# One 512-column product for the values of both residue groups, and the order of the first slots behind it

## The chip, the cores and the metric

The kernel runs on one core of a Trainium2 chip. The metric is device time in microseconds of one execution, the median of several runs; lower is better. The core's engines have these names in the profile: PE is TensorE (with PEld, its weight loads), DVE is VectorE, ACT is ScalarE, POOL is GpSimd, SP is SyncE. Each has its own instruction list and runs it in order; semaphores hold an instruction back until what it needs from another engine or a DMA is there.

## The reference

One layer of a hybrid decoder on x of 512 positions x 1024 channels, in float32. It normalizes x, multiplies it with one wide matrix W_in, and splits the result among three mixers, whose gated outputs are merged; a SwiGLU follows, and a last normalization. The change touches mixer A, dilated window attention of 12 heads in three groups of 4:

```python
A_GROUPS = ((128, 1), (512, 4), (2048, 16))
for g, (window, dilation) in enumerate(A_GROUPS):
    sl = slice(g * A_HEADS_PER_GROUP, (g + 1) * A_HEADS_PER_GROUP)
    o, lse = dilated_window_attention(qa[:, :, sl], ka[:, :, sl], va[:, :, sl],
                                      dilation, window // dilation, rel_bias[:, sl])
    ...
wts = jax.nn.softmax(jnp.stack(lses, axis=0), axis=0)
o_a = jnp.sum(wts[..., None] * jnp.stack(outs, axis=0), axis=0)
```

Group 0 sees the last 128 positions. Groups 1 and 2 gather keys at stride 4 and 16. Head j of each group is combined with head j of the others through the softmax denominators.

## The kernel before

The layer runs as one long list of matmuls, with the transposed activations x (8 tiles of 128 channels x 512 positions) kept in SBUF. Every float32 product is three matmuls in a rounded format: a number is a high part plus a rest, and `mm3` (L195) adds high x high, low x high and high x low. So x stands as xhi and xlo, a weight chunk of 128 x 1024 as whi and wlo. `stage_g` (L164) brings a chunk: SyncE loads wraw, ScalarE casts whi, and GpSimd (for most chunks) or VectorE subtracts wlo. `chunk_plan` (L56) lists the chunks in the order in which the products take them, two ahead of use.

A projection (`project`, L225; `fa`, L663) holds the weights still and lets the 512 positions pass: 8 x 3 matmuls of 512 columns. `fa(half, i, w)` computes queries (w=0) or keys (w=1) of a pair of heads, and `q_tiles` (L470) and `k_tiles` (L492) split them into the tiles qh, ql, qq and kk on ScalarE and VectorE; with `scaled` false they first multiply by the norm (qt, kt: `unscaled`, L462). In `values_g` (L410) it is x that is held still and the 256 columns of a group's value weights that pass: 4 position blocks x 8 x 3 = 96 matmuls of 256 columns. VA[0] takes contiguous positions. VA[1] and VA[2] need the positions by residue class, every fourth one: `by_class` (L406) reads x at stride 4 as weights. `values_out` (L429) splits the values into v tiles.

A slot is one head j of the three groups. `la(j)` gives its steps of logits (`class_logits` L556 for groups 1 and 2, `head_logits` L522 for group 0); `weave` (L200) sets such steps between the matmuls of a product. `wa(d)` (L690) takes the exponentials on ScalarE and sends the statistics through DRAM (exch): ScalarE's queue issues the stores, SyncE's the loads that bring them back transposed. `wa2(d)` (L709) combines them on VectorE (mm, df, wd, ds, rd, ff) and scales P. `ta(d)` gives steps that transpose P (ph, pl and pp tiles), and `xa(d)` multiplies P with the values (L647, L765). `renorm` (L909) scales a second copy of x (xt) and splits it (hi, lo) into XN, the normalized x which later projections take. The order of all of it around the change is written out by hand in the list at L940 to L966; each engine's instruction order follows from a scheduler that works on it.

Of the kernel before, what the change touches and what calls it, by code (L numbers as in the profile page):

```python
# [30 lines left out]
OFF_QA, OFF_KA, OFF_VA = 0, A_W, 2 * A_W  # L31
# [24 lines left out]
def chunk_plan():  # L56

    plan = []

    def a(h, i, w):  # L60
        plan.append(("ma", (OFF_QA, OFF_KA)[w], A_PAIRS[h][i]))

    def v(off, g):
        plan.extend(("v", off + g * 256, kh) for kh in range(2))

    def c(m, w):
        plan.append(("m", "w_in", (OFF_QC, OFF_KC)[w] + m * 128))

    def b(m):
        plan.append(("m", "w_in", OFF_XB + m * 128))  # L70
        plan.append(("m", "w_in", OFF_GB + m * 128))

    gates = [("m", "w_in", OFF_GT + n * D + m * 128) for m in range(8) for n in range(3)]

    def g(place):
        for _ in range(EARLY[place]):
            plan.append(gates.pop(0))

    for n in (0, 1):
        a(0, n, 0)  # L80
        a(0, n, 1)
    v(OFF_VA, 0)
    v(OFF_VA, 1)
    a(0, 2, 0)
    a(0, 2, 1)
    v(OFF_VA, 2)
    for n in range(2):
        a(1, n, 0)
        a(1, n, 1)
    a(1, 2, 0)  # L90
    g("a2")
    a(1, 2, 1)
    g("a3")
    v(OFF_VC, 0)
    g("v0")
    v(OFF_VC, 1)
    c(0, 0)
    g("v1")
    c(0, 1)
    g("c0")  # L100
    c(1, 0)
    c(1, 1)
    g("c1")
    for m in (2, 3):
        c(m, 0)
        g("l1" if m == 2 else "l3")
        c(m, 1)
        g("l2" if m == 2 else "l4")
    b(0)
    g("b0")  # L110
    plan.append(("lru",))
    for m in range(1, 4):
        b(m)
    g("b1")
    np_ = 0
    for m in range(8):
        while gates and 24 - len(gates) < 3 * m + 3 + G_LEAD:
            plan.append(gates.pop(0))
        while np_ * 8 < (m + 1) * 10:
            plan.append(("p", np_))  # L120
            np_ += 1
    for m in range(8):
        plan.append(("m", "w_out", m * 128))
    for m in range(FT):
        plan.append(("m", "w_gu", m * 128))
        plan.append(("m", "w_gu", FFN + m * 128))
    for k in range(FT):
        plan.append(("d", k))
    return plan


def layer_kernel(tc, x0p, xT, wts, tab, oneh, msk, idn, gfin, out):
    nc = tc.nc
    plan = chunk_plan()
    pos = [0]

    with (
# [17 lines left out]
        def bank(s="ps"):  # L155
            return pp.tile([128, 512], F32, name=uid(s), tag="ps")
# [38 lines left out]
        def mm3(o, lh, ll, rh, rl, start, stop):  # L195
            nc.tensor.matmul(o, lh, rh, start=start, stop=False)  # L196
            nc.tensor.matmul(o, lh, rl, start=False, stop=False)  # L197
            nc.tensor.matmul(o, ll, rh, start=False, stop=stop)  # L198

        def weave(gen, n, steps=(), first=0):  # L200

            done = 0
            i = 0
            while True:
                try:
                    next(gen)
                except StopIteration as e:
                    for st in steps[done:]:
                        st()
                    return e.value  # L210
                i += 1
                while done < len(steps) and i - first >= (done + 1) * (n - first) / (len(steps) + 1):
                    steps[done]()
                    done += 1
# [51 lines left out]
        X = []  # L266
        parts = [stage_g(), stage_g()]
        for k in range(KT):
# [8 lines left out]
            g = xp[:, 512 + k : 513 + k]  # L277
            hi = slot(F32R, "xhi")
            nc.scalar.activation(hi, xt, AF.Copy, scale=g)
            lo = slot(F32R, "xlo")  # L280
# [125 lines left out]
        def by_class(ap):  # L406

            return ap.rearrange("p (i c) -> p c i", c=4)

        def values_g(perm=False, act=X):  # L410
            ch = [chunk("v"), chunk("v")]
            pss = []
            for tb in range(4):
                if tb % 2 == 0:
                    pss.append(bank())
                o = pss[-1][:, (tb % 2) * 256 : (tb % 2) * 256 + 256]
                t = slice(tb * 128, (tb + 1) * 128)
                for k in range(8):
                    hi, lo = ch[k // 4]
                    c = slice((k % 4) * 256, (k % 4) * 256 + 256)  # L420
                    xs = [by_class(x)[:, tb, :] if perm else x[:, t] for x in act[k]]
                    mm3(o, xs[0], xs[1], hi[:, c], lo[:, c], k == 0, k == 7)
                    yield
            return pss

        def values_mm(steps=(), first=0, perm=False, act=X):
            return weave(values_g(perm, act), 32, steps, first)

        def values_out(pss, perm=False, scaled=False):  # L429
            res = []  # L430
            for tb in range(4):
                o = pss[tb // 2][:, (tb % 2) * 256 : (tb % 2) * 256 + 256]
                o4 = o.rearrange("p (h e) -> p h e", h=4)
                v = slot(F32R, "v")
                v4 = v.rearrange("p (h two e) -> p h two e", two=2, e=E)
                if scaled:
                    nc.scalar.copy(v4[:, :, 0, :], o4)
                    nc.vector.tensor_sub(v4[:, :, 1, :], o4, f32(v4[:, :, 0, :]))
                    res.append(v)
                    continue  # L440
                rt = r_tok[:, tb + 4 * perm : tb + 4 * perm + 1]
                nc.scalar.activation(v4[:, :, 0, :], o4, AF.Copy, scale=rt)
                nc.vector.scalar_tensor_tensor(
                    v4[:, :, 1, :], in0=o4, scalar=rt, in1=f32(v4[:, :, 0, :]),
                    op0=ALU.mult, op1=ALU.subtract,
                )
                res.append(v)
            return res
# [212 lines left out]
                qk[pair[n] + (w,)] = t[n]  # L661

        def fa(half, i, w, steps=(), first=0):  # L663
            scaled = half == 1
            ea(project(XN if scaled else X, "ma", steps, first), half, i, w, scaled)

        def st_part(st, s, o):
# [241 lines left out]
        def renorm(ks):  # L909
            for k in ks:  # L910
                xt = x_again[k]
                nc.vector.scalar_tensor_tensor(xt, in0=xt, scalar=prm[:, k : k + 1], in1=rb,
                                               op0=ALU.mult, op1=ALU.mult)
                XN.append(split(xt))
# [25 lines left out]
        VA.append(values_out(weave(va0, 32)))  # L940
        reload()
        d0, st = la(0)
        VA.append(values_out(values_mm(st, 0, True), True))
        wa(d0)
        renorm(range(4))
        fa(0, 2, 0)
        renorm(range(4, 8))
        fa(0, 2, 1)
        wa2(d0)
        d1, st = la(1)  # L950
        VA.append(values_out(values_mm(st, 8, True), True))
        st = ta(d0)
        fa(1, 0, 0, st)
        wa(d1)
        fa(1, 0, 1)
        xa(d0)
        fa(1, 1, 0)
        wa2(d1)
        fa(1, 1, 1)
        st = ta(d1)  # L960
# [283 lines left out]
def _pack_weights(inp):  # L1244
    f = np.float32
    w = {n: np.asarray(inp[n])[0] for n in ("w_in", "w_out", "w_gu", "w_down", "p_a", "p_b", "p_c")}
    pk = []
    for m in range(8):
        for n in ("p_a", "p_c", "p_b"):
            a = w[n][:, m * 128 : m * 128 + 128]  # L1250
            pk.extend(a[k * 128 : k * 128 + 128] for k in range(a.shape[0] // 128))
    plan = chunk_plan()
    out = np.zeros((len(plan), 128, 1024), f)
    for i, c in enumerate(plan):
        if c[0] == "v":
            _, off, kh = c
            a = w["w_in"][kh * 512 : kh * 512 + 512, off : off + 256]
            out[i] = a.reshape(4, 128, 256).transpose(1, 0, 2).reshape(128, 1024)
        elif c[0] in ("m", "ma"):
            if c[0] == "m":  # L1260
                a = w[c[1]][:, c[2] : c[2] + 128]
            else:
                a = np.concatenate(
                    [w["w_in"][:, c[1] + (g * 4 + j) * E : c[1] + (g * 4 + j + 1) * E] for g, j in c[2]],
                    axis=1,
                )
            out[i] = a.reshape(8, 128, 128).transpose(1, 0, 2).reshape(128, 1024)
        elif c[0] == "p":
            out[i] = np.concatenate(pk[c[1] * 8 : c[1] * 8 + 8], axis=1)
        elif c[0] == "lru":  # L1270
            for wi, n in enumerate(("lru_wa", "lru_wx")):
                a = np.asarray(inp[n])[0]
                for b in range(8):
                    r, t = (b % 2) * 64, wi * 512 + (b // 2) * 128
                    out[i, r : r + 64, t + r : t + r + 64] = a[b]
        else:
            out[i] = w["w_down"][c[1] * 128 : c[1] * 128 + 128]
    return out
# [41 lines left out]
```

## Time and profile before

| what | value |
|---|---|
| median of 3 runs | 917.45 us (917.18 to 918.51) |
| the profiled execution | 919.07 us |
| its span (first to last instruction) | 917.3 us |
| TensorE busy | 897.8 us, 98% |
| VectorE, ScalarE, GpSimd busy | 473.7, 398.5, 244.4 us |
| HBM | 98 GB/s over the span |

The profiled execution lies 1.6 us above the median, and 1.8 us of its time lie outside its span. Times within the span are counted from its start. Matmuls overlap one another in the records, so the spacing of their starts says what one costs.

### The profile page before, as it was taken

To read this page: it belongs to the slowest core of one execution; us is meant where nothing else is said; L and a number is where in the kernel's file an instruction comes from. 1 tells how busy PE (TensorE), PEld (TensorE's weight loads), DVE (VectorE), ACT (ScalarE), POOL (GpSimd) and SP (SyncE) were. 2 spreads that over 40 slices of the span, in tenths; PEclk is the share of its full clock that TensorE was granted. 3 is DMA by queue.
4 is the path that set the end of the run, shared out by engine and by line. 5 is a ranking of instruction groups with operands and counts; after the bars stand their busy time and mean duration, and the time that the engine had idled before them with its cause. 6 is when DMAs were issued, how large, how long until landed. Compare 5 with 4: busy or idle time off the path is not lost.

```text
span 917.3 us, 11267 instructions
## 1 busy us (share of the span) xinstructions
PE 897.8 (98%) x4262; PEld 760.7 (83%) x4262; DVE 473.7 (52%) x922; ACT 398.5 (43%) x692; POOL 244.4 (27%) x163
## 2 busy tenths in 40 slices
PE   9999699999999999999999999999999999999996
PEld 7899688998888888878888888888888888888885
DVE  7497766634655666745334544544444444422226
ACT  7356457546666567763223433333232223211113
POOL 1124045337443333456112130211111111100004
PEclk9899799999999999999999999999999999999998
DMA  7243132362322231223322332322222232222302
GB/s 277 80 149 90 42 116 71 104 105 102 109 89 91 78 107 50 88 101 107 104 88 106 118 111 71 100 97 96 98 92 93 93 111 95 93 92 97 110 24 92
DMA packets 40278, 90.27 MB, mean 98 GB/s; under 512 B 13988, under 2 KB 15780, under 8 KB 40224
## 3 DMA queue, kind: packets, MB, share of 16 engines
q1 hardware_dynamic: 34048, 88.26, 29.2%
q10 hardware_dynamic: 5824, 0.98, 0.7%
q8 instruction: 33, 0.54, 0.3%
q0 software_dynamic: 352, 0.33, 0.1%
q14 instruction: 21, 0.17, 0.1%
HBM read 87.34 MB, written 2.20 MB: 98 GB/s over the span
## 4 chain that ended last, share of the span: by engine, by line
PE 88%; DVE 6%; ACT 4%; DMA 1%; issue 1%; DVEq 0%
PE ps L197 23%; PE ps L196 23%; PE ps L198 23%; PE ps L1171 11%; PE ps L647 1%; PE ps L596 1%; DVE gb L886 1%; PE ps L542 1%; PE ps L543 1%; DVE a L881 1%; ACT whi L178 1%; DMA stn<-exch 1%; DVE xc L840 0%; DVE y L1216 0%; ACT junk L1202 0%
## 5 line engine op out<-in xcount | busy, mean ns | idle before, releaser
L178 ACT CAST whi<-wraw 128x1024 fp32r<-128x1024 f32 (+1 forms) x149 | 154.6, 1039 | 279.6 <-issue 104.9
L196 PE MATMUL ps<-hi,whi 128*128 128x512 f32 x520 | 205.6, 396 | 1.1 <-ACT hi L248 1.1
L197 PE MATMUL ps<-lo,whi 128*128 128x512 f32 x520 | 202.8, 390 | 0.2 <-DVE lo L249 0.2
L198 PE MATMUL ps<-hi,wlo 128*128 128x512 f32 x520 | 202.8, 390 | 0.0
L179 POOL TENSOR_TENSOR wlo<-wraw,whi 128x1024 fp32r<-128x1024 f32 x55 | 133.9, 2437 | 234.4 <-ACT whi L178 225.8
L179 DVE TENSOR_TENSOR wlo<-wraw,whi 128x1024 fp32r<-128x1024 f32 (+1 forms) x94 | 116.9, 1244 | 123.9 <-ACT whi L178 123.8
L196 PE MATMUL ps<-uhi,whi 128*128 128x512 f32 x352 | 137.9, 392 | 0.0
L198 PE MATMUL ps<-uhi,wlo 128*128 128x512 f32 x352 | 137.1, 389 | 0.0
L197 PE MATMUL ps<-ulo,whi 128*128 128x512 f32 x352 | 136.9, 389 | 0.0
L198 PEld LDWEIGHTS ps<-hi,wlo 128*128 128x128 f32 x520 | 97.6, 188 | 20.8
L196 PEld LDWEIGHTS ps<-hi,whi 128*128 128x128 f32 x520 | 97.7, 188 | 20.1 <-ACT hi L248 1.5
L197 PEld LDWEIGHTS ps<-lo,whi 128*128 128x128 f32 x520 | 97.8, 188 | 19.1 <-DVE lo L249 0.5
L1145 POOL TENSOR_TENSOR av<-sg,uu 128x512 f32<-128x512 f32 x22 | 45.7, 2079 | 198.5 <-DVE sg L1143 198.5
L198 PEld LDWEIGHTS ps<-uhi,wlo 128*128 128x128 f32 x352 | 66.1, 188 | 13.9
L197 PEld LDWEIGHTS ps<-ulo,whi 128*128 128x128 f32 x352 | 66.1, 188 | 13.6
L196 PEld LDWEIGHTS ps<-uhi,whi 128*128 128x128 f32 x352 | 66.1, 188 | 13.3
L1171 PE MATMUL ps<-whi,lo 128*128 128x512 f32 (+1 forms) x180 | 57.7, 384 | 0.0
L1171 PE MATMUL ps<-wlo,hi 128*128 128x512 f32 (+1 forms) x180 | 57.6, 384 | 0.0
L1171 PE MATMUL ps<-whi,hi 128*128 128x512 f32 (+1 forms) x180 | 57.2, 384 | 0.0
L1141 DVE TENSOR_TENSOR uu<-ps,rb 128x512 f32<-128x512 f32 x22 | 15.2, 690 | 64.9 <-PE ps L198 64.9
L1171 PEld LDWEIGHTS ps<-whi,hi 128*128 128x128 f32 x180 | 33.8, 188 | 6.8
L1171 PEld LDWEIGHTS ps<-wlo,hi 128*128 128x128 f32 x180 | 33.8, 188 | 6.7
(240 smaller groups left out, 1292.1 us busy)
## 6 DMA issues: line engine op xcount, KB each, us to landing
wraw<-in_wts SPq DMA_DIRECT2D x145, 512.0 KB, 3.2
xt<-in_xT SPq DMA_DIRECT2D x15, 256.0 KB, 5.6
bias<-relb SPq DMA_DIRECT2D x8, 256.0 KB, 5.1
xr<-in_xT SPq DMA_DIRECT2D x8, 256.0 KB, 2.6
out<-y SPq DMA_DIRECT2D x7, 256.0 KB, 2.1
wraw<-in_wts SPq DMA_DIRECT2D x4, 256.0 KB, 4.9
bias<-relb SPq DMA_DIRECT2D x4, 128.0 KB, 4.1
bias<-relb SPq DMA_DIRECT2D x8, 64.0 KB, 4.8
```

The source lines that it names most:

```text
L178: nc.scalar.copy(hi[:, cc], raw[:, cc])
L179: eng.tensor_sub(lo[:, cc], raw[:, cc], f32(hi[:, cc]))
L196: nc.tensor.matmul(o, lh, rh, start=start, stop=False)
L197: nc.tensor.matmul(o, lh, rl, start=False, stop=False)
L198: nc.tensor.matmul(o, ll, rh, start=False, stop=stop)
L542: nc.tensor.matmul(bk, qh[:, qc], kk[:, k0 : k0 + nn], start=True, stop=False)
L543: nc.tensor.matmul(bk, ql[:, qc], kk[:, k0 : k0 + nn], start=False, stop=True)
L596: nc.tensor.transpose(bt[:, o : o + 128], p, ident)
L647: nc.tensor.matmul(po[:, o0 : o0 + n], vf(kt), p, start=(i == 0), stop=(i == len(mms) - 1))
L1141: nc.vector.tensor_mul(uu, pu, r2)
L1145: nc.gpsimd.tensor_mul(av, sg, uu)
L1171: nc.tensor.matmul((acc[tb][hf] if o is None else o)[:, cc], l[:, t], r[:, hf * 512 + cc.start : hf * 512 + cc.stop], start=((k == 0 or fi ...
```

## The change

The values of groups 1 and 2 become one product, `class_values_g`. Its weights are chunks of a new kind, "vv": 256 input channels x 512 columns (both groups side by side), four chunks of the same size as before; the two chunks that VA[2] took after fa(0,2,1) are taken here. For each tile k of x the four residue classes are held still in turn, and 512 columns pass into four PSUM banks, one per class: 8 x 4 x 3 = 96 matmuls of 512 columns instead of 2 x 96 of 256. The steps of slot 0's logits are woven into it as they were into VA[1].

The order of the first slots changes with it. VA[2] no longer stands behind fa(0,2,1), so the steps of slot 1's logits are woven into fa(1,0,0) (from its fourth matmul group on); fa(1,0,0) and fa(1,0,1) take the unnormalized X, with the two multiplies qt and kt that go with it; all eight tiles of `renorm` follow wa2(d0); and xa(d0) comes after fa(1,1,0).

```diff
     v(OFF_VA, 0)
-    v(OFF_VA, 1)
+    plan.extend(("vv", OFF_VA + 256, kq) for kq in range(4))
     a(0, 2, 0)
     a(0, 2, 1)
-    v(OFF_VA, 2)
...
+        def class_values_g():
+
+            pss = [bank() for _ in range(4)]
+            for kq in range(4):
+                hi, lo = chunk("vv")
+                for k in (2 * kq, 2 * kq + 1):
+                    c = slice((k % 2) * 512, (k % 2) * 512 + 512)
+                    for tb in range(4):
+                        xs = [by_class(x)[:, tb, :] for x in X[k]]
+                        mm3(pss[tb], xs[0], xs[1], hi[:, c], lo[:, c], k == 0, k == 7)
+                        yield
+            return [[ps[:, g * 256 : g * 256 + 256] for ps in pss] for g in range(2)]
...
         def fa(half, i, w, steps=(), first=0):
-            scaled = half == 1
+            scaled = (half, i) > (1, 0)
...
         d0, st = la(0)
-        VA.append(values_out(values_mm(st, 0, True), True))
+        for outs in weave(class_values_g(), 32, st):
+            VA.append(values_out(outs, True))
         wa(d0)
-        renorm(range(4))
         fa(0, 2, 0)
-        renorm(range(4, 8))
         fa(0, 2, 1)
         wa2(d0)
+        renorm(range(8))
         d1, st = la(1)
-        VA.append(values_out(values_mm(st, 8, True), True))
+        fa(1, 0, 0, st, 3)
+        wa(d1)
         st = ta(d0)
-        fa(1, 0, 0, st)
-        wa(d1)
-        fa(1, 0, 1)
+        fa(1, 0, 1, st)
+        fa(1, 1, 0)
         xa(d0)
-        fa(1, 1, 0)
         wa2(d1)
         fa(1, 1, 1)
```

Three places show what this does to the engines' lists. The first is TensorE's list at the start of the product; before, it held one PSUM tile for one residue class and went through x (tiles xhi_104, xhi_110 and so on):

```order
L196 MATMUL ps_598<-whi_319,xhi_104 128x256
L197 MATMUL ps_598<-wlo_320,xhi_104 128x256
L198 MATMUL ps_598<-whi_319,xlo_106 128x256
L196 MATMUL ps_598<-whi_319,xhi_110 128x256
L197 MATMUL ps_598<-wlo_320,xhi_110 128x256
L198 MATMUL ps_598<-whi_319,xlo_112 128x256
```

Now the same place holds (ps_586 to ps_589 are the four banks of the four classes):

```order
L195 MATMUL ps_586<-whi_319,xhi_104 128x512
L196 MATMUL ps_586<-wlo_320,xhi_104 128x512
L197 MATMUL ps_586<-whi_319,xlo_106 128x512
L195 MATMUL ps_586<-whi_319,xhi_110 128x512
L196 MATMUL ps_586<-wlo_320,xhi_110 128x512
L195 MATMUL ps_587<-whi_319,xhi_104 128x512
L196 MATMUL ps_587<-wlo_320,xhi_104 128x512
L197 MATMUL ps_587<-whi_319,xlo_106 128x512
```

Each matmul passes twice the columns, and the banks are filled in turn, so that all four end at the product's end. The second place is TensorE's list where slot 1's logits begin (kk_889 before, kk_875 now). Before, half of VA[2] still follows them:

```order
L198 MATMUL ps_959<-whi_857,xlo_154 128x256
L542 MATMUL ps_1006<-kk_889,qh_827 128x256
L543 MATMUL ps_1006<-kk_889,ql_828 128x256
...
L543 MATMUL ps_1007<-kk_889,ql_828 128x256
L196 MATMUL ps_1026<-whi_795,xhi_104 128x256
```

Now fa(1,0,0) (ps_979) has ended ahead of them, and all logits of the slot follow, then fa(1,0,1) (ps_1087):

```order
L197 MATMUL ps_979<-xhi_152,wlo_802 128x512
L554 MATMUL ps_999<-kk_875,qh_833 128x256
L555 MATMUL ps_999<-kk_875,ql_834 128x256
...
L555 MATMUL ps_1000<-kk_875,ql_834 128x256
L576 MATMUL ps_1019<-kk_878,qq_839 128x256 x2
L576 MATMUL ps_1025<-kk_883,qq_839 128x256 x2
L576 MATMUL ps_1037<-kk_457,qq_442 128x256 x2
L576 MATMUL ps_1043<-kk_462,qq_442 128x256 x2
L195 MATMUL ps_1087<-xhi_104,whi_843 128x512
```

No product is left to fill in between the steps of the logits. The third place is VectorE's list at slot 1's exchange, where mm is the first step that needs it and the pp tiles are transposed P of slot 0, which TensorE takes in xa(d0):

```order
L612 TENSOR_TENSOR pl_1114<-ps_1109,ph_1113 128x384
L629 TENSOR_TENSOR pp_1127<-ps_1122,pp_1127 128x2x128
L725 TENSOR_TENSOR mm_1238<-stn_970 128x4
L725 TENSOR_TENSOR mm_1257<-stp_971 128x4
L727 TENSOR_TENSOR df_1240<-mm_1238,stn_970 128x4
L728 TENSOR_TENSOR df_1240<-mm_1238,stn_970 128x4
L727 TENSOR_TENSOR df_1259<-mm_1257,stp_971 128x4
L629 TENSOR_TENSOR pp_1130<-ps_1122,pp_1130 128x2x128
L728 TENSOR_TENSOR df_1259<-mm_1257,stp_971 128x4
L629 TENSOR_TENSOR pp_1144<-ps_1139,pp_1144 128x2x128
```

One pp tile is ahead of mm and the others behind it, as before; now the matmuls that take them stand on TensorE behind fa(1,1,0) and in front of nearly all of fa(1,1,1).

## Rows read from the trace of the kernel before

**Rows 1.** The page's first part: busy us (share of span) and instructions of each engine:

```profile
PE 897.8 (98%) x4262; PEld 760.7 (83%) x4262; DVE 473.7 (52%) x922; ACT 398.5 (43%) x692; POOL 244.4 (27%) x163
```

**Rows 2.** The waits of TensorE: us in total, times, longest us:

```profile
PE ps L542 <- DVE kk L512: 8.0, 1, 8.0
```

**Rows 3.** Stretches: us, busy us (x instructions) by engine, granted clock, DMA share, GB/s:

```profile
84.80:104.10 19.30, 11.25 (x50) 11.08 (x49) 14.54 (x41) 11.37 (x24) 2.38 (x1) 0.81 0.20 55
104.10:107.40 3.30, 3.30 (x15) 3.30 (x16) 3.21 (x9) 0.88 (x4) 0.00 (x0) 0.54 0.00 0
107.40:163.60 56.20, 56.20 (x282) 48.94 (x282) 34.49 (x114) 32.70 (x82) 22.78 (x16) 1.00 0.30 89
```

**Rows 4.** The chain that ended last, 86 to 105: start us, us, what:

```profile
86.66 2.54 DMA exch<-stp
...
89.21 4.65 DMA stn<-exch
...
104.09 0.55 PE ps L542
```

**Rows 5.** The timelines of VectorE and ScalarE's queue, 109 to 130: start us, us, what [idle before]:

```profile
109.35 0.89 DVE L567 TENSOR_TENSOR P<-ps,bias 128x256 f32<-128x256 f32 x2 [1.50 <-PE ps L564]
...
113.79 0.75 DVE L567 TENSOR_TENSOR P<-ps,bias 128x256 f32<-128x256 f32 x2 [2.71 <-PE ps L564]
...
120.58 0.37 ACTq L705 DMA_DIRECT2D exch<-stp  x1
...
127.72 1.05 DVE L713 TENSOR_TENSOR mm<-stn 128x4 f32<-128x4 f32 x1 [3.99 <-DMA stn<-exch]
...
129.11 0.75 DVE L617 TENSOR_TENSOR pp<-ps,pp 128x256 fp32r<-128x256 f32 x2
```

**Rows 6.** TensorE's timeline, 49 to 56:

```profile
49.43 0.28 PE L198 MATMUL ps<-whi,xlo 128*128 128x256 f32 x1
49.55 0.39 PE L196 MATMUL ps<-whi,xhi 128*128 128x256 f32 x1
49.78 0.40 PE L197 MATMUL ps<-wlo,xhi 128*128 128x256 f32 x1
...
55.15 0.28 PE L542 MATMUL ps<-kk,qh 128*128 128x256 f32 x1
```

**Rows 7.** Groups of weight loads, 28 to 123: count | busy us, mean ns:

```profile
L198 PEld LDWEIGHTS ps<-whi,xlo 128*128 128x128 f32 x96 | 28.6, 298 | 0.0
...
L197 PEld LDWEIGHTS ps<-xlo,whi 128*128 128x128 f32 x17 | 3.2, 188 | 0.6
```

**Rows 8.** VectorE's timeline, 62 to 100:

```profile
62.15 0.48 DVE L443 SCALAR_TENSOR_TENSOR v<-ps,mixr,v 128x256 fp32r<-128x256 f32 x1
...
64.99 2.06 DVE L912 SCALAR_TENSOR_TENSOR xt<-xt,prm,rb 128x512 f32<-128x512 f32 x3
...
72.20 0.42 DVE L567 TENSOR_TENSOR P<-ps,bias 128x256 f32<-128x256 f32 x1 [2.62 <-PE ps L564]
72.54 2.59 DVE L912 SCALAR_TENSOR_TENSOR xt<-xt,prm,rb 128x512 f32<-128x512 f32 x1
...
90.89 0.68 DVE L467 TENSOR_TENSOR qt<-ps,rq 128x512 f32<-128x512 f32 x1
...
98.79 0.68 DVE L246 TENSOR_TENSOR lo<-xt,hi 128x512 fp32r<-128x512 f32 x1
```

**Rows 9.** GpSimd's timeline, 72 to 117:

```profile
72.19 2.40 POOL L179 TENSOR_TENSOR wlo<-wraw,whi 128x1024 fp32r<-128x1024 f32 x1 [11.73 <-ACT whi L178]
...
116.61 2.39 POOL L179 TENSOR_TENSOR wlo<-wraw,whi 128x1024 fp32r<-128x1024 f32 x1 [26.79 <-ACT whi L178]
```

**Rows 10.** TensorE's timeline, 132 to 164:

```profile
132.58 0.40 PE L196 MATMUL ps<-hi,whi 128*128 128x512 f32 x1
...
138.05 0.39 PE L196 MATMUL ps<-hi,whi 128*128 128x512 f32 x1
...
163.57 0.28 PE L647 MATMUL ps<-ph,v 128*128 128x256 f32 x1
```

More of the change, by code (lines that the diff above doesn't have):

```diff
@@ L408, in by_class, with values_g @@
             return ap.rearrange("p (i c) -> p c i", c=4)
-        def values_g(perm=False, act=X):
+        def class_values_g():
[9 more added lines that the diff above has]
+            return [[ps[:, g * 256 : g * 256 + 256] for ps in pss] for g in range(2)]
+        def values_g(act=X):
             ch = [chunk("v"), chunk("v")]
-            pss = []
+            outs = []
             for tb in range(4):
                 if tb % 2 == 0:
-                    pss.append(bank())
-                o = pss[-1][:, (tb % 2) * 256 : (tb % 2) * 256 + 256]
+                    ps = bank()
+                o = ps[:, (tb % 2) * 256 : (tb % 2) * 256 + 256]
+                outs.append(o)
                 t = slice(tb * 128, (tb + 1) * 128)
@@ L420, in values_g, with values_mm, values_out @@
                     c = slice((k % 4) * 256, (k % 4) * 256 + 256)
-                    xs = [by_class(x)[:, tb, :] if perm else x[:, t] for x in act[k]]
-                    mm3(o, xs[0], xs[1], hi[:, c], lo[:, c], k == 0, k == 7)
+                    xh, xl = act[k]
+                    mm3(o, xh[:, t], xl[:, t], hi[:, c], lo[:, c], k == 0, k == 7)
                     yield
[L424 to L429, printed above, removed]
+            return outs
+        def values_mm(steps=(), first=0, act=X):
+            return weave(values_g(act), 32, steps, first)
+        def values_out(outs, perm=False, scaled=False):
             res = []
-            for tb in range(4):
-                o = pss[tb // 2][:, (tb % 2) * 256 : (tb % 2) * 256 + 256]
+            for tb, o in enumerate(outs):
                 o4 = o.rearrange("p (h e) -> p h e", h=4)
@@ L1258, in _pack_weights @@
             out[i] = a.reshape(4, 128, 256).transpose(1, 0, 2).reshape(128, 1024)
+        elif c[0] == "vv":
+            _, off, kq = c
+            a = w["w_in"][kq * 256 : kq * 256 + 256, off : off + 512]
+            out[i] = a.reshape(2, 128, 512).transpose(1, 0, 2).reshape(128, 1024)
         elif c[0] in ("m", "ma"):
```

## The prediction

> **What bounds the kernel now.** I read the page's first part, the list of what TensorE waited for, the stretches with their granted clock, the chain of waits and the timelines of each engine, in that order. TensorE is busy for 98% of the span [rows 1], and in the list of its waits only one is long, 8.0 us in one piece for a kk tile of VectorE [rows 2]. Everything else is TensorE running its list, so a change can win in two ways: shorten that list, or shorten the wait. The stretches show where both lie: in 84.80 to 104.10 TensorE is busy for 11.25 of 19.30 us, at a granted clock of 0.81; the next 3.30 us run at 0.54, close to the lower of the two levels (1.2 GHz); then 1.00 (2.4 GHz) without a wait up to 163.60 [rows 3]. The first 49.55 us of TensorE's list and all of it from xa(d1) on (163.57 us) are the same in both kernels, so the sum is made between these points.
>
> The wait belongs to a chain of small steps off TensorE. Slot 0's exponentials end, ScalarE issues exch<-stp at 86.66, SyncE reads it back at 89.21, it lands 4.65 later, at 93.86, VectorE starts mm, and its list from there ends in the kk tile that TensorE takes at 104.09 [rows 4]. A second round follows: exch<-stp at 120.58, mm at 127.72, the first pp tile behind it at 129.11 [rows 5]. TensorE had other work then and did not wait.
>
> **Part 1, the product.** Before, groups 1 and 2 take 2 x 96 matmuls of 256 columns with x taken at stride 4 as weights; 24 of them stand between 49.55 and 55.15, 0.233 us each, where 256 columns on contiguous weights need 0.12 (49.43 to 49.55) [rows 6] and 512 columns 0.228 (24 between 132.58 and 138.05) [rows 10]. The reason stands in the weight loads: 298 ns where x is taken by class, 188 where it is contiguous [rows 7]. So the stride, not the columns, paces them, and 512 columns can pass in the time in which 256 do. Now 96 matmuls of 512 columns do both groups. Lower bound of their spacing 0.233 us (the load stays the pace); upper bound 0.341, if the 0.108 us that 256 more columns take (0.228 less 0.12) came on top. I take the lower: on contiguous weights the load hides wholly. TensorE's list then shortens by 96 x 0.233 = **22.4 us** (12.0 at the upper bound).
>
> TensorE: Matmul & The Clock Gate in the Trainium skill (Part 3, The mechanism) speaks against that: weight loads overlap running matmuls only where their row groups differ. By that rule the product would cost the upper bound, 32.7 us and not 22.4. The contiguous rows, 188 ns of load at a spacing of 0.12, do not agree; the case has its chance among the rivals.
>
> **Part 2, the chain to the wait.** The two exchanges stay, in the same order behind each other, so the saving counts only as far as they move. Slot 0's logits are still woven into the product. Before, VectorE got the last of them after 2.62 us of waiting, at 72.20, and its next xt took 2.59 us where a free one takes 0.69 (2.06 for three), for GpSimd's wlo ran from 72.19 for 2.40 [rows 8, 9]: a VectorE step on two SBUF tensors stands still beside one, at a price of up to 1.9 us. After, the last logits come about as early, one more wlo falls beside the xt steps (+1.9), and three v steps of 0.48 and two lo steps leave the stretch (-2.8). I take the issue of exch<-stp as 0.9 us earlier, 85.8, between 84.7 and 86.7; mm 7.2 later [rows 4], **93.0**.
>
> From mm to TensorE it took 10.2 us. Out of it go four lo steps of 0.68 [rows 8] (-2.7; the change puts all eight behind the kk tiles); in come three v's of 0.48 (+1.4) and qt, 0.68 (+0.7). That is 9.6. But two wlo now fall in it, whose casts stand between ScalarE's steps there; before, GpSimd was idle for 26.79 us up to 116.61 [rows 9]. They cost 0 to 3.8; I take 2.4, a little over one. TensorE restarts at **105.0** (102.3 to 107.3), against 104.09. It has then done the whole product, fa(0,2,0), fa(0,2,1) and fa(1,0,0), and has stood for some 12 us (done at 49.55 + 22.4 + 1.9 of slot 0's logits + 3 of waits inside + 3 x 5.47 = 93.3). Before, half of the product for group 2 and fa(1,0,0) still lay ahead.
>
> **Part 3, slot 1's exchange.** From TensorE's restart to the issue of exch<-stp it took 16.5 us [rows 4, 5]. In come the eight lo steps ahead of the logits (+5.4) and qt (+0.7); out goes VectorE's wait for logits woven into the product, 1.50 and 2.71 (-4.2) [rows 5]. That is 18.4, plus one wlo beside the lo steps, 0 to 1.9, of which I take 0.6: 19.0. Issue at **124.0** (120.7 to 127.6), mm 7.1 later at 131.1 and the second pp tile 1.8 behind mm, at **132.9**. Here lies the new wait: xa(d0) needs that tile, which VectorE's list now puts behind mm, and fa(1,1,1) stands behind it on TensorE. fa(1,0,1) ends near 114; fa(1,1,0) can start when slot 1's logits are reduced, 12.9 behind the restart, and TensorE reaches xa(d0) at about 124.4: a wait of 8.5.
>
> **Part 4, on to xa(d1).** fa(1,1,1) began at 138.05 and xa(d1) at 163.57, 25.5 us of work without a wait [rows 10]; six matmuls of xa(d0) come on top (+0.7). After its new wait TensorE runs some 3.3 us at the lower level, as behind the wait of now [rows 3], which loses half of that, 1.6. So 132.9 + 25.5 + 0.7 + 1.6 = 160.7, against 163.57: **-2.9 us**. VectorE's own list keeps up: behind mm it has ql and qq fewer than now, which are done by then, and kt more. The two extra multiplies (2 x 0.68) are the qt above and a kt behind mm, beside TensorE's wait. Weight chunks keep their number and bytes and come two ahead of use, so I cost them at nothing; a late one would hold TensorE within the product, and the wait at 105 would swallow that. Slot 0's later logits take PSUM banks that v steps and earlier logits must free: about 3 us of waits within the product, swallowed in the same way.
>
> **Sum.** -22.4 for the product; +3.0 of waits inside it; +3.8 for the longer wait at 105 (11.8 for 8.0); +2.3 ahead of fa(1,1,0); +8.5 ahead of fa(1,1,1) and +1.6 for the slow start behind it: -3.2, and with the steps rounded above -2.9. The profiled execution took 919.07 us (span 917.3), which gives 916.2; it is 1.6 above the median of the runs, 917.45, so the median becomes **914.5**.
>
> **The rivals.**
> - *GpSimd's wlo miss VectorE.* All of them at nothing and an early issue: restart 102.3, second pp 129.6, xa(d1) at 157.4, 6.2 us gained: 911.3; and 906 if the eight lo steps (5.4) too fall beside other waits. For it: the xt row shows the stall where a step reads two SBUF tensors, and half of VectorE's steps there read PSUM. Against: the casts stand just where they collide.
> - *The whole saving arrives*, 895. That needs slot 0's exchange some 20 us earlier, and from its issue to mm alone go 7. Hardly.
> - *Everything is given back.* All wlo collide: restart 107.3, second pp 136.5, xa(d1) at 164.3, 0.7 later: 918.2, no change that can be told.
> - *Slower: strided weights don't hide behind 512 columns.* The last logits of slot 0 stand behind 72 class matmuls; at 0.341 they come 72 x 0.108 = 7.8 us later, of which the bank waits ahead of them swallow 2. Everything from exch<-stp on is 5.8 later: -2.9 becomes +2.9, 920.3. The gain is gone from a spacing of 0.30 us on, where 72 x 0.067 is 4.9. For it: no row shows a strided load under 512 columns, and its 298 ns are longer than the 228 that they take. Against: contiguous loads of 188 hide under 120.
> - *The change does not do what it says*: the order of instructions shows 96 matmuls fewer, so no.
>
> **How the numbers follow.** A run tells 0.2% from no change, 1.8 us. Forecast (gain of 1.8 to 6) 0.39, wlo missing (6 to 13) 0.18, whole saving 0.04: faster 0.61. Given back, within 1.8: 0.21. Slower 0.18. The range leaves out the whole saving and what lies beyond the ends worked out: 906 (wlo missing, lo steps covered) to 920.5 (strided loads at the upper bound).
>
> **What would show it.** Spacing in the product: 0.23 (right) or towards 0.34. TensorE's waits: one of about 12 us for kk, to near 105, and a second of 5 to 9 ahead of fa(1,1,1), for a pp tile, near 133; the wait for slot 0's v's in the product under 3. exch<-stp near 86 and 124. TensorE busy about 22 us less at a span only 3 shorter. The forecast is wrong if the second wait is missing, if exch<-stp of slot 0 moves by over 3 us, or if a wait after xa(d1) takes the gain.

## The result, and the profile after

| what | before | after |
|---|---|---|
| median | 917.45 us (917.18 to 918.51) | 924.43 us (923.98 to 924.81) |
| ratio to before, 95% interval | | 1.0074 [1.0056, 1.0091] |
| the profiled execution, its span | 919.07, 917.3 us | 924.81, 923.0 us |

The kernel became slower by 0.74%, 7.0 us. Forecast were 914.5 and a range that ended at 920.5. The page's first part after the change, to be held against [rows 1]:

```profile
PE 886.4 (96%) x4166; PEld 744.6 (81%) x4166; DVE 480.8 (52%) x924; ACT 400.6 (43%) x692; POOL 245.9 (27%) x163
```

TensorE has 96 matmuls fewer and is busy 11.4 us less, in a span that is 5.7 us longer. Its timeline in the product (start us, us, what):

```profile
53.14 0.40 PE L197 MATMUL ps<-whi,xlo 128*128 128x512 f32 x1
53.38 0.39 PE L196 MATMUL ps<-wlo,xhi 128*128 128x512 f32 x1
...
77.86 0.39 PE L197 MATMUL ps<-whi,xlo 128*128 128x512 f32 x1
78.09 0.39 PE L195 MATMUL ps<-xhi,whi 128*128 128x512 f32 x1
```

The starts are 0.235 us apart, against 0.233 for 256 columns [rows 6]: the product itself costs half of what it did, and it ends at 78.09. The loads of its strided weights, 49 to 78 (count | busy us, mean ns), are no faster than before (298, [rows 7]) and hide behind the 512 columns:

```profile
L196 PEld LDWEIGHTS ps<-wlo,xhi 128*128 128x128 f32 x31 | 9.7, 313 | 0.2
```

Where the gain went stands in the list of TensorE's waits (total us, times, longest us), to be held against the single 8.0 of [rows 2]:

```profile
PE ps L554 <- DVE kk L524: 12.1, 1, 12.1
PE ps L777 <- DVE df L728: 5.0, 1, 5.0
PE ps L576 <- DVE v L455: 3.1, 1, 3.1
PE ps L576 <- ACT z L907: 2.6, 1, 2.6
...
PE ps L576 <- DVE half L770: 1.0, 1, 1.0
```

The stretches after (us, busy us of each engine, granted clock, DMA share, GB/s) answer to [rows 3]:

```profile
64.14:67.60 3.46, 3.46 (x10) 2.74 (x9) 2.73 (x3) 2.92 (x4) 3.06 (x2) 0.51 1.05 400
...
94.60:106.71 12.11, 0.00 (x0) 0.03 (x1) 11.19 (x22) 5.09 (x8) 5.34 (x2) 0.66 0.25 87
106.71:115.20 8.49, 7.93 (x25) 6.67 (x26) 7.86 (x10) 6.99 (x12) 2.82 (x1) 0.50 0.00 0
...
129.60:134.55 4.95, 0.00 (x0) 0.03 (x1) 0.98 (x8) 0.48 (x3) 1.26 (x1) 0.79 0.69 207
134.55:139.20 4.65, 4.65 (x12) 3.68 (x13) 4.57 (x20) 4.05 (x8) 0.00 (x0) 0.50 0.02 7
139.20:163.21 24.01, 24.01 (x124) 20.32 (x123) 15.80 (x41) 13.92 (x31) 10.65 (x9) 1.00 0.18 67
163.21:182.00 18.79, 17.64 (x124) 16.26 (x122) 7.50 (x32) 9.56 (x30) 4.80 (x2) 1.00 0.45 99
182.00:190.00 8.00, 5.41 (x31) 5.17 (x32) 8.00 (x35) 2.86 (x9) 3.17 (x4) 0.82 0.00 0
```

Two things are to be seen. Up to xa(d1) the gain is spent: waits of 21.8 us for 8.0, and three starts at the lower level (1.2 GHz, 0.50 to 0.51 in the rows: 3.5, 8.5 and 4.65 us, about half of which is lost) for one of 3.3. That is 13.8 and some 6.5 against the product's 22; xa(d1) begins at 163.21, 0.36 earlier than before [rows 10]. And behind xa(d1), where the kernel before has no wait, TensorE stands for 3.7 us, and its clock sinks to 0.82 for 8. The timeline of VectorE there, before and after:

```profile
171.55 0.68 DVE L758 TENSOR_TENSOR half<-ps,half 64x512 f32<-64x512 f32 x1
172.16 1.27 DVE L769 TENSOR_TENSOR hp<-ps,hp 64x512 f32<-64x512 f32 x2
177.10 0.53 DVE L713 TENSOR_TENSOR mm<-stn 128x4 f32<-128x4 f32 x1 [3.67 <-DMA stn<-exch]
```

```profile
180.32 0.16 DVE L725 TENSOR_TENSOR mm<-stn 128x4 f32<-128x4 f32 x1 [7.10 <-DMA stn<-exch]
180.40 0.16 DVE L725 TENSOR_TENSOR mm<-stp 128x4 f32<-128x4 f32 x1
180.59 0.68 DVE L770 TENSOR_TENSOR half<-ps,half 64x512 f32<-64x512 f32 x1
181.27 0.68 DVE L781 TENSOR_TENSOR hp<-ps,hp 64x512 f32<-64x512 f32 x1
```

Before, half and hp of xa(d1) run when TensorE has their products, and mm of slot 2 waits for its exchange behind them. After, mm stands ahead of them, and they wait 9 us for an exchange that they don't need. They free PSUM banks that TensorE takes at 181.33, and GpSimd's and ScalarE's steps behind them (oa, hi, z) hold it once more at 186.75. No line of the diff touches slot 2: the scheduler that turns the program into instruction lists put mm there. In the profiles the stretch from xa(d1) to xa(d2) takes 56.33 us for 50.31; from xa(d2) to the end they agree, 703.49 for 703.42.

### The profile page after: what moved, and what is told of

Its sections match the earlier page's. It is cut to its first block, busy times and chain, and to the rows that moved or that the text cites. A ratio compares the mean times of both kernels' runs of the same rounds, so it can differ in the third digit from the quotient of the medians.

```text
span 923.0 us, 11073 instructions
## 1 busy us (share of the span) xinstructions
PE 886.4 (96%) x4166; PEld 744.6 (81%) x4166; DVE 480.8 (52%) x924; ACT 400.6 (43%) x692; POOL 245.9 (27%) x163
## 4 chain that ended last, share of the span: by engine, by line
PE 76%; DVE 9%; ACT 5%; DMA 5%; issue 4%; POOL 0%; DVEq 0%; ACTq 0%; POOLq 0%; SPq 0%
PE ps L196 20%; PE ps L195 20%; PE ps L197 20%; PE ps L1182 11%; DMA exch<-stp 2%; ACT P L594 1%; PE ps L608 1%; PE ps L659 1%; DMA stn<-exch 1%; DVE xt L924 1%; DVE gb L898 1%; DVE lo L245 1%; PE ps L555 1%; DMA xt<-in_xT 1%; PE ps L554 1%
## 5 line engine op out<-in xcount | busy, mean ns | idle before, releaser
L195 PE MATMUL ps<-hi,whi 128*128 128x512 f32 x504 | 200.2, 398 | 1.1 <-ACT hi L247 1.1
L196 PE MATMUL ps<-lo,whi 128*128 128x512 f32 x504 | 197.6, 392 | 0.2 <-DVE lo L248 0.2
L197 PE MATMUL ps<-hi,wlo 128*128 128x512 f32 x504 | 197.3, 391 | 0.0
L195 PEld LDWEIGHTS ps<-hi,whi 128*128 128x128 f32 x504 | 95.4, 189 | 20.0 <-ACT hi L247 1.6
L197 PEld LDWEIGHTS ps<-hi,wlo 128*128 128x128 f32 x504 | 95.3, 189 | 20.2
L196 PEld LDWEIGHTS ps<-lo,whi 128*128 128x128 f32 x504 | 95.5, 189 | 18.9 <-DVE lo L248 0.5
L1182 PEld LDWEIGHTS ps<-whi,lo 128*128 128x128 f32 x180 | 33.8, 188 | 6.8
```

The lines of the kernel that those rows point to most:

```text
L1182: nc.tensor.matmul((acc[tb][hf] if o is None else o)[:, cc], l[:, t], r[:, hf * 512 + cc.start : hf * 512 + cc.stop], start=((k == 0 or fi ...
```

## The experiments

Every ratio is to the kernel before, measured beside it on the same chip; edits that build on one another were in part measured on different chips. One profile of an execution is less certain than a ratio: the same lists of TensorE and VectorE up to xa(d1) reached it at 159.8 us on one chip and at 164.3 on another (both_first, slot2_load_both).

**Theory A:** the change moves the bound of the first slots from TensorE to VectorE and the two exchanges, and the order that came with it costs more behind xa(d1). **Rivals:** the product itself is at fault, or what is lost behind xa(d1) would be lost in any order.

### VectorE's order at slot 2

`half_first`: wa2(d2) of the changed kernel behind the last hp of xa(d1) in VectorE's list; TensorE's list is left alone.

```diff
+                tail[0] = nc.vector.tensor_add(hp, pc[0:64, :], hp)
...
-        wa2(d2)
+        with tc.issue_after(tail[0].ins):
+            wa2(d2)
```

> The changed kernel with one edge more: VectorE may issue the mm of slot 2's exchange only behind the half and hp steps of xa(d1). TensorE's list is the same. Theory A (the 6 us behind xa(d1) come from VectorE's order: half and hp stand behind an mm that waits for the exchange until 180.3): half runs near 173, TensorE's waits for half (1.0) and hp (0.2) are gone, that for z shrinks from 2.6 to under 1.5, and the time falls by 5 to 7 us, to 917.5 to 919.5. Theory B (the exchange itself, 11.1 us from issue to mm where it was 8.8 before, is what costs, through the P steps and z behind mm): the time falls by 2 us at most, 922 to 925.

Ratio 1.0019 [1.0009, 1.0029]: 0.55% or 5.0 us of the 0.74% are gone. VectorE:

```profile
172.20 0.68 DVE L771 TENSOR_TENSOR half<-ps,half 64x512 f32<-64x512 f32 x1
172.81 1.27 DVE L782 TENSOR_TENSOR hp<-ps,hp 64x512 f32<-64x512 f32 x2
179.85 0.16 DVE L725 TENSOR_TENSOR mm<-stn 128x4 f32<-128x4 f32 x1 [5.78 <-DMA stn<-exch]
```

`before_mm_first` is the mirror: in the kernel before, wa2(d2) is written ahead of xa(d1), and an order-only dependency puts half and hp behind mm of slot 2. Up to xa(d1), VectorE's order stays as it was.

> The mirror of half_first: the kernel before, with slot 2's mm of VectorE put ahead of half and hp of xa(d1), the order that the change had brought with it; TensorE's list is left alone. Theory A (the order at slot 2 costs by itself): half waits for mm, some 177.1 us instead of 171.6, TensorE stalls behind it by 1 to 3.5 us in the stretch 175 to 190, and the time is 1 to 4 us over the kernel before. Rival (the order is harmless where TensorE has the product's 22 us still in it): no difference, within 0.5 us.

Ratio 1.0050 [1.0035, 1.0065]: 4.6 us slower, a little more than expected, without a trace of the change's product. VectorE and then the stretch 182 to 190 look as in the changed kernel:

```profile
179.18 0.16 DVE L713 TENSOR_TENSOR mm<-stn 128x4 f32<-128x4 f32 x1 [6.45 <-DMA stn<-exch]
...
179.45 0.68 DVE L758 TENSOR_TENSOR half<-ps,half 64x512 f32<-64x512 f32 x1
```

```profile
182.00:190.00 8.00, 5.92 (x35) 5.43 (x34) 8.00 (x37) 3.23 (x11) 2.39 (x3) 0.80 0.00 1
```

That is some two thirds of the loss by the ratios: taking the order away gives 5.0 us back, bringing it in alone costs 4.6. In the profiles, 3.6 and 3.9 of it lie between xa(d1) and xa(d2) (56.33 to 52.75, and 50.31 to 54.23), where the order differs; some 1 us lies ahead of xa(d1), where it doesn't. So the order's own price is 3.6 to 5 us.

### The second wait, at slot 1

`pp_first` puts wa2(d1) behind the last pp tile in the same way; `both_first` has both edits.

> The changed kernel with another edge: VectorE may issue the mm of slot 1's exchange only behind the four pp steps of slot 0. The order at slot 2 stays that of the changed kernel. Theory A: TensorE's wait of 5.0 at 134.55 goes, fa(1,1,1) starts near 130.5 and not at 134.6; but slot 1's mm does not come sooner, so VectorE's list behind it stays where it is, TensorE waits later by most of what it won, xa(d1) comes 0.5 to 2 us sooner, and the loss at slot 2 stays: 922 to 924.5. Rival (the 5.0 us are what the change lost): 918.5 to 920.5.

> Both edges together. Theory A: 916 to 919, the gain of half_first and up to 2 us of pp_first. Rival (each wait only hands its time to the next one): not below 921.

1.0065 [1.0046, 1.0085] and 1.0002 [0.9992, 1.0012]. The 5.0 us wait is gone in both, but 0.8 us of time (against the changed kernel, which the intervals don't tell from nothing) and 1.6 (both_first against half_first) are all that comes of it. In pp_first, where slot 2's order is still the new one, TensorE waits 2.4 us for slot 1's P (from 141 us on) and 0.8 for pp tiles instead, and half of xa(d1) runs at 180.04, as late as without the edit.

### The product alone, and the sequence alone

`two_passes`: the changed kernel, but 256 columns at a time, weights passing twice.

```diff
+                        for g in range(2):
+                            c = slice((k % 2) * 512 + g * 256, (k % 2) * 512 + g * 256 + 256)
+                            mm3(pss[tb][:, g * 256 : g * 256 + 256], xs[0], xs[1], hi[:, c], lo[:, c],
+                                k == 0 and g == 0, k == 7 and g == 1)
```

> The changed kernel with the class values' product cut back into two passes of 256 columns, weights passing twice, all else (staging, banks, the sequence of the first slots) as changed; to be held against the changed kernel (924.4 us where the kernel before has 917.5). Theory A (the product's 22 us do pay within the changed sequence, and the new sequence loses more than that): the product ends some 20 us later (96 to 101 instead of 78.1), the logits of slot 1 start 8 to 15 us later than 106.7, and the time is 8 to 18 us over the changed kernel. Rival (the 22 us are hidden in any order): within 3 us of the changed kernel.

Ratio 1.0142 [1.0127, 1.0158]: 0.68% or 6.2 us above the changed kernel, between the two expectations. The product's last matmul begins at 96.08, 18.2 us later, slot 1's logits at 114.78, 8.1 later. The other 10 us stand in the wait at kk, which is 2.0 us where the changed kernel has 12.1; the second wait stays:

```profile
PE ps L779 <- DVE df L730: 5.4, 1, 5.4
...
PE ps L556 <- DVE kk L526: 2.0, 1, 2.0
```

So the change is the sum of two parts: a sequence that costs 1.42% (13 us, the order at slot 2 among them), and a product that gives 0.68% of it back. The product is not at fault.

`xn_renorm_split` keeps the product and puts back two more pieces of the old sequence: `renorm` in halves ahead of fa(0,2,0) and fa(0,2,1), and fa(1,0,·) on the normalized x. Slot 2's order on VectorE comes out as before with it.

```diff
-            scaled = (half, i) > (1, 0)
+            scaled = half == 1
...
+        renorm(range(4))
         fa(0, 2, 0)
+        renorm(range(4, 8))
         fa(0, 2, 1)
         wa2(d0)
-        renorm(range(8))
```

> The changed kernel with a part of the new sequence undone: the eight xt and lo steps again in two halves around fa(0,2,0), and fa(1,0,0) and fa(1,0,1) on the normalized XN, so without the two extra multiplies; the product of 512 columns stays. VectorE's order at slot 2 comes out as half, hp, mm here. Theory A: the eight lo steps (7.1 us between 109.8 and 116.9) leave the chain from TensorE's restart to slot 1's exchange and go into waits before it, slot 1's exchange is issued 3 to 7 us sooner, and with the order at slot 2 right the time is 912 to 917. Rival (the lo steps only move ahead and delay the kk tile by as much): 917 to 920.

Ratio 0.9993 [0.9983, 1.0004]. TensorE now waits 10.5 us for lo tiles, in three pieces, and 2.9 for a hi, where it waited for kk. With the order mended in this way too, a product that is 22 us shorter is worth under 2 us.

### What holds the first slots

`kk_first`: on half_first, VectorE's work that waits for slot 0's exchange stands behind the kk tiles of fa(0,2,1). `before_kk_first`: the same edit in the kernel before.

```diff
-        wa2(d0)
+        with tc.issue_after(last_kk[0].ins):
+            wa2(d0)
```

> On top of half_first: wa2(d0), VectorE's work that waits for slot 0's exchange, stands behind the last kk of fa(0,2,1) in VectorE's list, not ahead of it; TensorE's list is left alone. Theory A (what bounds the stretch is the exchange of slot 0 through VectorE's queue, and the product's saving was turned into the 12.1 us wait at kk): that wait falls to under 2 us, the logits of slot 1 start at 94.6 to 97 instead of 106.2, the store of slot 1's exchange is issued 6 to 10 us earlier (117 to 121), and the time falls by 5 to 11 us against half_first, below the kernel before. Rival (the wait is only handed on, to the eight lo that fa(1,1,0) needs or to slot 1's own exchange): one of those waits grows to 8 us or more and the time moves by less than 2 us.

> The same edge in the kernel before: wa2(d0) behind the last kk of fa(0,2,1). There TensorE waits 8.0 us at kk. Theory A (both kernels are held by slot 0's exchange through kk, the change more so): the wait goes and the time falls by 3 to 8 us against the kernel before, and kk_first ends 3 to 10 us below this kernel, because only then the product's shorter TensorE work counts. Rival (the product's saving is worth nothing in any order): kk_first and this kernel end within 2 us of each other, or kk_first above.

0.9982 [0.9971, 0.9993] and 0.9953 [0.9939, 0.9966], on the same chip. TensorE's longest waits in kk_first:

```profile
PE ps L611 <- issue: 7.0, 1, 7.0
PE ps L781 <- DVE pp L632: 2.4, 2, 1.7
PE ps L625 <- DVE P L602: 2.2, 2, 1.9
```

and in before_kk_first:

```profile
PE ps L545 <- DVE kk L515: 3.7, 1, 3.7
PE ps L196 <- DVE stn L553: 1.5, 1, 1.5
```

The wait at kk falls from 11.7 to 0.9, as theory A had it, and the time by 3.4 us, less than it had. The rest is handed on to the transposes of slot 0's P (L611). The profile names no releaser for that wait; TensorE ends it at 111.56, just behind VectorE's first steps on slot 1's logits (111.04 to 111.46), which stand behind its scaling of slot 0's P (104.98 to 109.70) and two lo steps. So VectorE's list holds TensorE there too; which tile of it isn't shown. The kernel before gains more by the same edit, 4.3 us, and ends 2.7 us *below* kk_first: the second rival of that pair. With slot 0's exchange out of the way on both sides, the change still loses. From slot 0's store to slot 1's it takes 33.9 us in the kernel before (86.66 to 120.58, [rows 4, 5]), 43.4 after the change (83.24 to 126.59), 37.3 in kk_first and 29.6 in before_kk_first. The 9.4 us that the change adds are 1.9 from the store to mm, 4.2 from mm to TensorE's restart and 3.4 from there to slot 1's store. The reading that fits, argued from the lists and not tried by itself: before, two of renorm's eight lo and half of the v tiles ran ahead of slot 0's store and the other six lo ahead of kk, while now all of them lie between the two stores, the lo behind kk; and TensorE has no product left to fill in there.

`renorm_early`, `renorm_early_kk`: on half_first and on kk_first, `renorm` in halves ahead of fa(0,2,0) and fa(0,2,1). `lo_pool_kk`: kk_first with the eight lo of `renorm` on GpSimd.

> On top of half_first: the renormalised x is split in two halves ahead of fa(0,2,0) and fa(0,2,1), where the kernel before has it, not behind wa2(d0). Theory A (the eight lo in 109.8 to 116.9, between TensorE's restart and slot 1's softmax, are what makes slot 1's exchange late): they run ahead of kk, slot 1's store is issued 3 to 7 us earlier than in half_first (119 to 123 instead of 126.1), the wait at L777's line falls to under 2 us, and the time falls by 2 to 5 us. Rival (VectorE's work is only shifted to ahead of kk): the wait at kk grows from 11.7 to 15 us or more and the time moves by less than 1.5 us.

> renorm_early and kk_first together: VectorE has v, lo and kk ahead of the work that waits for slot 0's exchange. Theory A (the stretch is bound by VectorE's list, and the best order fills its idle 86 to 92 us): kk ends by 100, slot 1's store is issued at 114 to 118, and the time is 2 to 6 us below kk_first. Rival (the list is full in any order): store at 119 or later and time within 1.5 us of kk_first.

> kk_first with the eight lo of the renormalised x computed by GpSimd instead of VectorE (0.65 us each on VectorE). Theory A (VectorE's list bounds the stretch 83 to 117 us): some 5 us leave it, slot 1's store is issued 3 to 5 us earlier than 120.6, and the time falls by 1 to 4 us against kk_first. Rival (GpSimd's lo come later than fa(1,1,0) needs them, or slow VectorE beside them): TensorE waits 3 us or more for lo, and the time is that of kk_first or above.

1.0016 [1.0003, 1.0029], 0.9999 [0.9989, 1.0009] and 0.9989 [0.998, 0.9999]: none faster than its base, as the rivals had it; renorm_early_kk ends 1.6 us above kk_first, and in lo_pool_kk the 3 us wait for lo, which the rival named too, is missing. In renorm_early the wait at kk grows to 19.3 us, for the lo steps now stand ahead of it. In lo_pool_kk the lo steps leave VectorE, but its scaling of P takes 4.2 us longer, most of what they took (timelines of VectorE in kk_first, then in lo_pool_kk with its GpSimd):

```profile
104.98 4.72 DVE L602 TENSOR_SCALAR P<-P,ff 128x128 f32<-128x128 f32 x12
```

```profile
102.31 8.89 DVE L602 TENSOR_SCALAR P<-P,ff 128x128 f32<-128x128 f32 x12
```

```profile
102.32 2.41 POOL L178 TENSOR_TENSOR wlo<-wraw,whi 128x1024 fp32r<-128x1024 f32 x1
104.69 5.06 POOL L245 TENSOR_TENSOR lo<-xt,hi 128x512 fp32r<-128x512 f32 x4
```

Slot 1's store goes out at 120.89, no earlier than kk_first's 120.59. None of the three shortened the stretch between the two stores further than kk_first had.

### Bulk loads beside the exchanges

`hold_load`: on half_first, the 512 KB weight load that SyncE issued between slot 0's two exchange loads goes behind both (an order-only dependency on its own queue).

> On top of half_first: the 512 KB weight load that SyncE issued between slot 0's two exchange loads (83.1 us) is issued behind both. Theory A (the weight load beside it lengthens the exchange store from 2.5 to 6.4 us): the store lands within 2.5 to 4.0 us, mm of slot 0 runs at 89 to 90.5 instead of 91.8, TensorE restarts at 103 to 105 instead of 106.2, and the time falls by 1 to 3 us against half_first. Rival (the flight is the store's own, or set by other loads): the store still takes over 5.5 us, restart and time as in half_first within 0.7 us.

Ratio 1.0014 [1.0002, 1.0026], no difference to half_first. The chain of waits in half_first, then in hold_load:

```profile
83.19 6.19 DMA exch<-stp
89.44 2.36 DMA stn<-exch
```

```profile
81.83 4.43 DMA exch<-stp
86.28 2.41 DMA stn<-exch
```

The store lands 1.8 us faster, not as fast as the 2.54 of [rows 4]; mm comes 3.1 us earlier, 1.4 of it because the store was issued earlier, and the wait ahead of fa(1,1,1) grows from 4.9 to 5.9. So, as far as one profile shows it, the load was some of the store's delay, and the chain passes little of it on.

From xa(d1) to xa(d2) TensorE took 50.3 us in the profile of before (163.57 to 213.87) and 52 to 56 in all others, before_kk_first too (52.8). `slot2_load`, `slot2_load_both`, `slot2_load_before_kk` and `slot2_load_kk` hold the load beside slot 2's exchange in the same way, on half_first, both_first, before_kk_first and kk_first.

> On top of half_first: the 512 KB weight load that SyncE issues between slot 2's two exchange loads (172.6 us) is issued behind both. From xa(d1) to xa(d2) TensorE takes 50.3 us in the kernel before and 52.8 in half_first; slot 2's second exchange store lands 4.1 us after its issue in the kernel before and 9.4 in half_first. Theory A (the weight load that runs beside the store delays it, and TensorE gives its lead back there): the store lands within 6 us, mm of slot 2 runs at 174 to 177.5 instead of 179.85, the 1.5 us wait of TensorE near 185 falls to under 0.5, xa(d1) to xa(d2) takes 50.3 to 51.5, and the time falls by 1.3 to 2.5 us against half_first. Rival (the store is late for its own small packets or the next wait is another): mm after 178.5, 52 us or more from xa(d1) to xa(d2), no change of time.

> The same on top of both_first, where TensorE reaches xa(d1) at 159.8, 3.8 us ahead of the kernel before, and still ends with it. Theory A: xa(d2) comes at 210.1 to 211.3 instead of 213.7, and the time is 2 to 3.5 us under the kernel before, what the prediction gave (-2.9). Rival: xa(d2) at 213 or later, no difference to the kernel before.

> The same on top of before_kk_first, which gave back 2.5 us between xa(d1) and xa(d2) too (52.8 for 50.3) without any of the change. Theory A: 50.3 to 51.5 there, and 1.3 to 2.5 us less than before_kk_first. Rival: no difference.

> The same on top of kk_first (54.2 us from xa(d1) to xa(d2)). Theory A: 50.3 to 52, and 2 to 3.5 us less than kk_first, so some 4 to 5 us under the kernel before. Rival: no difference to kk_first.

1.0026 [1.0015, 1.0037], 1.0003 [0.999, 1.0016], 0.9989 [0.9976, 1.0002] and 0.9978 [0.9963, 0.9993]. Theory A falls: slot 2's store still took 10.35, 9.56, 7.00 and 9.73 us, and TensorE 52.7 to 54.9 from xa(d1) to xa(d2). Three times match their bases; on before_kk_first it even cost 0.36%, though mm came at 172.05 for 176.32: a wait of 2.5 us for z stands where waits of 0.5 and 1.5 stood. What makes that store slow stays open. Where the 2 to 3 us go between xa(d1) and xa(d2) is in the lists of waits: before, TensorE has none there, and in half_first two, 1.9 of the 2.4 us that it takes longer than the kernel before (52.75 for 50.31):

```profile
PE ps L195 <- DVE stn L562: 1.5, 1, 1.5
PE ps L576 <- ACT z L908: 0.4, 1, 0.4
```

before_kk_first has the same two, 1.5 and 0.5, of 2.5 us.

## Why the prediction was wrong

**The failed step** is the first one, the frame of the sum: "the first 49.55 us of TensorE's list and all of it from xa(d1) on (163.57 us) are the same in both kernels, so the sum is made between these points". TensorE's list is the same there. VectorE's is not: mm of slot 2 had changed places with half and hp of xa(d1), and that costs 5.0 us (half_first) or 4.6 (before_mm_first) by the ratios. The sum looked behind xa(d1) at TensorE's order alone; VectorE's list would have shown the swap. The condition "if a wait after xa(d1) takes the gain" was named, without a chance and a price.

**The product** was right: 0.235 us a matmul, 22 us off TensorE's list. The rival of strided weights that don't hide is out: 0.341 would have been its spacing. The rule in TensorE: Matmul & The Clock Gate in the Trainium skill (Part 3, The mechanism), that weight loads overlap running matmuls only where the row groups differ, is not borne out by this trace, where loads of 313 ns hide at 0.235; the same section also lets a load into the background weight buffer run ahead, and no run here shows which buffer a load takes.

**The chain to the restart** was right in kind, and 1.7 us short: 106.71 for 105.0, behind a wait of 12.1 us for 11.8. The store went out at 83.24, 2.6 us earlier than forecast and 3.4 earlier than before, over the 3 us that the prediction had named as a sign of being wrong, but took 6.44 us to land where 2.54 had been taken over from [rows 4]; mm came at 92.34 (93.0). From mm on, 14.4 us for 12.0: two steps stood beside GpSimd's wlo, as the chain shows:

```profile
83.24 6.44 DMA exch<-stp
...
89.74 2.58 DMA stn<-exch
...
95.15 2.20 DVE ff L740 x2
...
99.39 2.73 DVE ql L469
```

ff takes 0.23 and one ql 0.69 without GpSimd beside them: 4.0 us for the 2.4 that were taken, a little over the upper bound of 3.8.

**Slot 1's exchange:** issue at 126.59 for 124.0, 0.9 us more from the restart on (the eight lo took 7.09 for 6.0). The second wait came where it was forecast, for VectorE's list behind mm, and was 5.0 for 8.5, because TensorE itself arrived later: 129.6 for 124.4, after 8.5 us at the lower level. That slow start cost nothing by itself: the second wait, which ended at 134.55 for 132.9, swallowed it. **On to xa(d1)** 28.7 us for 27.8, 0.7 of it because the lower level lasted 4.65 us there and not 3.3. In all 163.21 for 160.7: the terms between the two points were mis-sized by 2.5 us. Step by step they are 2.6 less for the earlier store, 1.9 more from it to mm (its flight 3.9 longer, the load back 2.1 shorter), 2.4 more to the restart, 0.9 more to slot 1's store, 0.9 less from there to the end of the second wait, and 0.9 more to xa(d1). Alone, the 2.5 would have given 917.0, inside the range. Of the 9.9 us between 914.5 and 924.4 these are 2.5, and 6.0 are lost between xa(d1) and xa(d2), most of them by the order at slot 2. 1.2 more come from the profiled executions: the one before lay 1.6 above its median, the one after 0.4. That leaves 0.1 behind xa(d2).

**What the forecast had no place for** is why even the mended orders don't gain. The gain was taken as 22 us less the new waits, as if waits could be worked off one by one. both_first and xn_renorm_split take them away at slots 1 and 2, kk_first takes away the longest of all, and each time much of the wait comes back at the next tile that VectorE owes. Between slot 0's and slot 1's exchange TensorE is no longer what bounds the kernel: of the product's 22 us, two_passes shows 6.2 in the time. TensorE was busy 11.4 us less where 22 had been named as a sign.

**The best version** is none of the change: before_kk_first, 0.9953 [0.9939, 0.9966] of the kernel before, under both kernels.

## What to carry to other kernels

Where a scheduler orders the engines, a change on one engine's list can change the others': compare every engine's order to the end of the program, not only up to where the edit's own engine is the same again. Work that fills an engine while a chain runs elsewhere has a second value, as cover; halving it gains little until the chain is shorter too (6.2 of 22 us in two_passes). And a step that waits for a transfer should stand in its engine's list behind all that is ready and free of it.

## What the runs showed of the hardware

- **GpSimd and VectorE.** Twelve steps that scale P took 2.63 us in the kernel before (at 179.63, GpSimd idle), 4.72 beside one wlo and 8.89 beside a wlo and four lo, 6.3 more than the 2.63 where GpSimd's own took 7.5 in all: VectorE stands still for most of the time that GpSimd runs. SBUF — State Buffer in the Trainium skill (SBUF: two separate sides) says that the two share a port pair as an exclusive lock, held for a whole instruction. These rows agree, for a VectorE step that reads one large SBUF tensor. That lo_pool_kk gained nothing fits this: its scaling of P is 4.2 us slower than kk_first's.
- **Small stores.** The same 4 KB store of statistics landed in 2.54 us at slot 0 of the kernel before [rows 4] and in 1.6 (two_passes) to 8.0 (slot2_load_both) in the others, and in 4.1 (before) to 10.5 (hold_load) at slot 2. A bulk load held back explains 1.8 us of it at slot 0, in one profile, and shortened it by 0.6 us at most at slot 2.
- **The clock after a wait.** Behind the 8.0 us wait of before, the granted clock was back within 3.3 us [rows 3]; behind the 5.0 us wait of after, after 4.65 us, and behind its 12.1 us wait only after 8.5 us, in which TensorE ran slot 1's logits and stood for 0.56 us once more. Half of that, 4 us of TensorE's time, is lost on top of the wait; here the second wait swallowed it.
